# Two encoder layers in one kernel: two more of eleven swiglu blocks by seven products, the other blocks divided into steps

## The chip, the cores and the metric

The kernel runs on one core of a Trainium2 chip. The metric is the device time of one execution in microseconds. Before the change the median of three runs was 2283.49 us (2281.22 to 2284.84).

## The reference

Two layers on 256 tokens of width 2048, all in float32. Layer 0 mixes tokens with chunked gated linear attention (GLA), layer 1 with an indexer and top-k attention (DSA); each mixer is followed by a swiglu whose inner width is 5632, and a last RMSNorm ends it.

```python
def swiglu(h, w1, w3, w2):
    return (jax.nn.silu(h @ w1) * (h @ w3)) @ w2

for i in range(DEPTH):
    x = x + mixer(rmsnorm(x, norm_mix[i]))
    x = x + swiglu(rmsnorm(x, norm_ffn[i]), ffn_w1[i], ffn_w3[i], ffn_w2[i])
return rmsnorm(x, norm_final)
```

## The kernel before, in words

**One product.** A float32 product is made of three passes in the type float32r: each operand is split into a high part and a rest, and high x high, high x rest and rest x high are added up in a PSUM bank. A weight tile of 512 rows by 512 columns (1 MB) is split by `split_w` (L132): ScalarE (ACT) casts it into `wh` (L136), VectorE (DVE) subtracts that from it into `wl` (L137). Both have three buffers. Raw weights come by SyncE's queue (SP) into `raw`, which has four. A chunk is what one such tile feeds.

**A swiglu block.** The inner width is cut into eleven blocks of 512 columns. The 256 tokens are two tiles of 128; the contraction over 2048 is cut into two halves. `plain` (L450) computes a block of w1 and then of w3 in eight chunks, 24 matmuls of 128x512 each, 192 in all (L464), into three PSUM banks of the pool `acc`. `pair` (L369) takes the same block of w1 and w3 as the two column halves of one matrix product and the token tiles and contraction halves as the others, so that the scheme of Strassen and Winograd gives it in seven products of 24 matmuls (L394), 168 in all. The products are named after the form of the activations that is stationary: A11, F5, F3, F6, F7, A12, N22. The weights change between products: `va` holds w1's first half, `vb` w3's. After A11 has split `va`, VectorE adds `vb` to it (`plus`, L406); after F5 has split that, a DMA adds w3's second half to it in place (`plus_dma`, L409, issued by POOL); F3 splits `vc`, w3's second half from `raw`, and adds it to `vb` (L406); F6 splits `va` and a second accumulating DMA adds w1's second half; F7 splits `vb`, A12 splits `vd`, w1's second half from `raw`, and N22 splits `va`. Every product goes by two chunks. `va` and `vb` live in two places that change roles from pair to pair (`homes`, `turn`, L413): the next pair's `va` is loaded where this pair's `vb` was, its `vb` where this pair's `va` was.

**Down projection.** `pieces` (L477) multiplies two finished blocks by w2, in eight steps of one chunk and 24 matmuls (L490 to L492), into two banks of the pool `ms`; after every second step VectorE adds both banks to x (L497).

**Order.** `ffn` (L500) runs b = 0 to 10. Blocks 2, 4, 6, 8 and 10 are pairs, the other six plain. `pair` yields after each product and once more at its end, and at each yield one step of the down projection of the two blocks before it runs; beside plain blocks none is left to run. A finished block is transposed by `split_t` (L209), which goes on the deque `side` and is taken up by `tick` between matmuls. What is left over, block 10, goes to `residual` (L348) after the swiglu, which multiplies it by w2 and, in layer 0, prepares the next layer; in layer 1 the last quarter of it is `gemm_tail` (L140), one token tile after the other, and the final norm follows.

A planner puts the instructions of each engine into one queue ahead of the run, in the program's order as far as its own costs say that operands and buffers are ready, and fills in the semaphores. So an instruction can stand before one that precedes it in the program.

Of the kernel before, what the change touches and what calls it, by code (L numbers as in the profile page):

```python
# [12 lines left out]
F32 = mybir.dt.float32  # L13
# [6 lines left out]
P = 128  # L20
SEQ = 256
# [34 lines left out]
def trunk(  # L56
# [38 lines left out]
    cols = cst.tile([P, 72], F32, name="cols")  # L95


    sm.tile([P, 24], F32, tag="pad", bufs=1, name="pad")

    def gains(c0, srcs):  # L100

# [262 lines left out]
    def flush():  # L364
        while side:
            tick()


    def pair(nrm, wa, wb, c0, turn, done):  # L369

        def src(w, j, c):
            r = j * 1024 + c * 512
            return w[r:r + 512, c0:c0 + NB].rearrange("(k p) n -> p k n", p=P)

        def load(w, j, homes):
            o = []
            for c, (pool, tag, bufs) in enumerate(homes):
                raw = pool.tile([P, 4, NB], F32, tag=tag, bufs=bufs, name=tag)  # L380
                nc.sync.dma_start(raw, src(w, j, c))
                o.append(raw)
            return o

        def product(acc, raws, form, start, stop, then=None):
            for c in range(2):
                wh, wl = split_w(raws[c])
                if then is not None:
                    then(c)
                hi, lo = nrm.forms[form]  # L390
                for j in range(4):
                    k = 4 * c + j
                    for i, (l_, r_) in enumerate(((hi, wh), (hi, wl), (lo, wh))):
                        nc.tensor.matmul(acc, l_[:, k, :], r_[:, j, :], start=start and k == i == 0,  # L394
                                         stop=stop and k == 7 and i == 2, skip_group_check=not start)
                    if j % 2:
                        tick()

        def bank():
            return acc_p.tile([P, NB], F32, tag="acc", name="acc")  # L400

        def sums(tag):
            return nrm.pool.tile([P, NB], F32, tag=tag, bufs=1, name=tag)

        def plus(dst, other):
            return lambda c: nc.vector.tensor_add(dst[c], dst[c], other[c])  # L406

        def plus_dma(dst, w, j):
            return lambda c: nc.gpsimd.dma_start(dst[c], src(w, j, c), accum_op=ALU.add)  # L409

        fz = nrm.pool
        stream = [(wp, "raw", RAW)] * 2
        homes = [((fz, "v0", 1), (fz, "v1", 1)), ((fz, "v2", 1), (res, "g3", 1))]  # L413
        va = load(wa, 0, homes[turn])
        vb = load(wb, 0, homes[1 - turn])
        b1 = bank()
        product(b1, va, "A11", True, True, plus(va, vb))
        s1 = sums("s1")
        nc.scalar.copy(s1, b1)
        yield  # L420
        b2 = bank()
        product(b2, va, "F5", True, True, plus_dma(va, wb, 1))
        y = sums("y")
        nc.vector.tensor_sub(y, b2, s1)
        yield
        vc = load(wb, 1, stream)
        product(b2, vc, "F3", False, True, plus(vb, vc))
        yield
        b3 = bank()
        product(b3, va, "F6", True, True, plus_dma(va, wa, 1))  # L430
        w = sums("w")
        nc.vector.tensor_sub(w, b3, s1)
        yield
        product(b3, vb, "F7", False, True)
        nc.vector.tensor_add(w, w, b2)
        nc.vector.tensor_add(y, y, b3)
        yield
        vd = load(wa, 1, stream)
        product(b1, vd, "A12", False, True)
        done("11", b1)  # L440
        done("12", w)
        yield
        product(b3, va, "N22", False, True)
        nc.vector.tensor_sub(s1, s1, b3)
        done("21", s1)
        done("22", y)
        yield
        yield

    def plain(nrm, ws, c0, done):  # L450

        for q, w in zip("12", ws):
            acc = [acc_p.tile([P, NB], F32, tag="acc", name="acc") for _ in range(3)]
            for g in range(4):
                raw = wp.tile([P, 4, NB], F32, tag="raw", bufs=RAW, name="raw")
                nc.sync.dma_start(raw, w[g * NB:(g + 1) * NB, c0:c0 + NB].rearrange("(k p) n -> p k n", p=P))
                wh, wl = split_w(raw)
                for bank, form, start, stop in ((0, "A11", True, True), (1, "F7", True, True)) if g < 2 else \
                        ((0, "A12", False, True), (2, "N22", True, True)):
                    hi, lo = nrm.forms[form]  # L460
                    for j in range(4):
                        k = 4 * (g % 2) + j
                        for i, (l_, r_) in enumerate(((hi, wh), (hi, wl), (lo, wh))):
                            nc.tensor.matmul(acc[bank], l_[:, k, :], r_[:, j, :], start=start and k == i == 0,  # L464
                                             stop=stop and k == 7 and i == 2, skip_group_check=not start)
                        if j % 2:
                            tick()
                if g == 1:
                    s1 = nrm.pool.tile([P, NB], F32, tag="s1", bufs=1, name="s1")
                    nc.scalar.copy(s1, acc[0])  # L470
                    nc.vector.tensor_add(s1, s1, acc[1])
                    yield
            nc.vector.tensor_sub(s1, s1, acc[2])
            done("1" + q, acc[0])
            done("2" + q, s1)

    def pieces(w, parts):  # L477

        for n in range(NG):
            acc = [ms_p.tile([P, NB], F32, tag="ms", name=f"down{t}") for t in range(NT)]  # L480
            for gi, (hi, lo, r0) in enumerate(parts):
                raw = wp.tile([P, 4, NB], F32, tag="raw", bufs=RAW, name="raw")
                nc.sync.dma_start(raw, w[r0:r0 + 512, n * NB:(n + 1) * NB].rearrange("(k p) n -> p k n", p=P))
                wh, wl = split_w(raw)
                for k in range(4):
                    start = gi == 0 and k == 0
                    last = gi == len(parts) - 1 and k == 3
                    for t in range(NT):
                        ts_ = slice(t * P, (t + 1) * P)
                        nc.tensor.matmul(acc[t], hi[:, k, ts_], wh[:, k, :], start=start, stop=False)  # L490
                        nc.tensor.matmul(acc[t], hi[:, k, ts_], wl[:, k, :], start=False, stop=False)  # L491
                        nc.tensor.matmul(acc[t], lo[:, k, ts_], wh[:, k, :], start=False, stop=last)  # L492
                    if k % 2:
                        tick()
                if gi == len(parts) - 1:
                    for t in range(NT):
                        nc.vector.tensor_add(x[t][n], x[t][n], acc[t])  # L497
                yield

    def ffn(layer, nrm):  # L500

        w1, w3, w2 = ffn_w1[layer], ffn_w3[layer], ffn_w2[layer]
        sc = {}
        parts = []
        down = deque()
        for b in range(DFF // NB):
            us = [None] * NT

            def done(q, v):
                t = int(q[0]) - 1  # L510
                if q[1] == "1":
                    us[t] = cm.tile([P, NB], F32, tag="u", name="u")
                    nc.scalar.activation(us[t], v, AF.Silu, scale=sc["r"][:, t:t + 1])
                else:
                    nc.vector.scalar_tensor_tensor(us[t], us[t], sc["r"][:, t:t + 1], v, op0=ALU.mult, op1=ALU.mult)

            for slot, _ in enumerate(pair(nrm, w1, w3, b * NB, b // 2 % 2, done) if b in range(2, 11, 2) else plain(nrm, (w1, w3), b * NB, done)):
                if b == 0 and slot == 0:
                    flush()
                    r = nrm.rstd()  # L520
                    sc["r"] = r
                while down:
                    try:
                        next(down[0])
                        break
                    except StopIteration:
                        down.popleft()
            hi, lo = hi_lo(b % 3)
            side.append(split_t(us, hi, lo))
            parts.append((hi, lo, b * NB))  # L530
            if b % 2:
                down.append(pieces(w2, parts))
                parts = []
        while down:
            for _ in down.popleft():
                pass
        return w2, parts


# [554 lines left out]
```

## Time and profile before

| | |
|---|---|
| median of three runs | 2283.49 us |
| the profiled execution | 2283.89 us |
| its span, first to last instruction | 2282.1 us |
| PE, DVE, ACT, POOL busy | 2254.4, 1499.3, 1127.5, 79.3 us |
| mean granted TensorE clock | 0.998 of full speed |
| moved by DMA | 468.18 MB, mean 205 GB/s |

PE is TensorE's matmuls, PEld its weight loads, SP SyncE's queue. A matmul's recorded duration is longer than the distance to the next start, since matmuls overlap; lengths of stretches are more reliable than sums of durations. A "releaser" is what ended a wait, told from semaphores.

### The profile page before, as it was taken

What the parts mean: (1) busy time and instruction counts of PE and PEld (TensorE: products, weight loads), DVE (VectorE), ACT (ScalarE), POOL (GpSimd) and SP (SyncE); (2) the same over time, 40 slices, a digit from 0 to 9 for tenths busy, and PEclk for the clock granted to TensorE, in tenths of its full rate; (3) what the DMA queues carried; (4) which work ended last, traced back from release to release, by engine and by line L of the source; (5) the groups of instructions that cost most, each with busy time, mean ns of one, the idle gap of its engine ahead of it and who ended that gap; (6) DMA issues with size and microseconds to landing.
All of it is one profiled execution on the core that took longest, in us unless ns stands there. A gap on an engine that the chain in (4) does not pass through costs nothing.

```text
span 2282.1 us, 25208 instructions
## 1 busy us (share of the span) xinstructions
PE 2254.4 (99%) x10343; PEld 1856.3 (81%) x10343; DVE 1499.3 (66%) x1254; ACT 1127.5 (49%) x1026; POOL 79.3 (3%) x131
## 2 busy tenths in 40 slices
PE   9999999999999999999999999999999999999998
PEld 7888888887888888887888888888888788888886
DVE  6546456577676867776655755556675867777676
ACT  5545355444454545545544544455454454545454
POOL 0000000000000000000100000000000000000000
PEclk9999999999999999999999999999999999999999
DMA  8555465759495876857554555457496786949593
GB/s 286 168 171 188 127 233 187 237 160 302 147 299 199 216 263 184 289 159 218 173 182 148 184 166 166 165 186 240 147 277 234 193 273 174 296 146 305 166 239 111
DMA packets 242098, 468.18 MB, mean 205 GB/s; under 512 B 7816, under 2 KB 20448, under 8 KB 241856
## 3 DMA queue, kind: packets, MB, share of 16 engines
q1 hardware_dynamic: 219856, 423.33, 54.4%
q0 software_dynamic: 21120, 41.95, 10.7%
q8 instruction: 81, 1.33, 0.2%
q10 hardware_dynamic: 1008, 1.31, 0.2%
q14 instruction: 33, 0.27, 0.0%
HBM read 464.43 MB, written 2.12 MB: 204 GB/s over the span
## 4 chain that ended last, share of the span: by engine, by line
PE 68%; issue 20%; DMA 5%; DVE 4%; ACT 2%; POOL 0%; POOLq 0%; ACTq 0%; SPq 0%
PE acc L464 14%; PE acc L204 11%; PE acc L202 11%; PE acc L203 11%; PE acc L394 8%; PE down L490 3%; PE down L491 3%; DMA g<-in_ffn_w 3%; PE down L492 3%; DVE wl L137 2%; DMA v<-in_ffn_w 2%; ACT wh L136 1%; DVE v L406 1%; PE tr L216 1%; PE trq L825 0%
## 5 line engine op out<-in xcount | busy, mean ns | idle before, releaser
L137 DVE TENSOR_TENSOR wl<-raw,wh 128x2048 fp32r<-128x2048 f32 x217 | 496.8, 2290 | 261.3 <-ACT wh L136 261.3
L136 ACT CAST wh<-raw 128x2048 fp32r<-128x2048 f32 x217 | 415.7, 1915 | 474.1 <-PE down L492 176.6
L193 DVE TENSOR_TENSOR wl<-raw,wh 128x2048 fp32r<-128x2048 f32 (+3 forms) x147 | 317.8, 2164 | 276.4 <-ACT wh L192 276.3
L192 ACT CAST wh<-raw 128x2048 fp32r<-128x2048 f32 (+3 forms) x147 | 265.5, 1809 | 230.8 <-PE acc L204 194.6
L202 PE MATMUL acc<-wh,hh 128*128 128x512 f32 (+3 forms) x832 | 326.8, 393 | 0.0
L204 PE MATMUL acc<-wh,hl 128*128 128x512 f32 (+3 forms) x832 | 318.4, 383 | 0.0
L203 PE MATMUL acc<-wl,hh 128*128 128x512 f32 (+3 forms) x832 | 317.0, 381 | 0.5 <-DVE wl L193 0.5
L491 PE MATMUL down<-wl,g 128*128 128x512 f32 x640 | 249.2, 389 | 0.0
L492 PE MATMUL down<-wh,g 128*128 128x512 f32 x640 | 249.0, 389 | 0.0
L490 PE MATMUL down<-wh,g 128*128 128x512 f32 x640 | 247.5, 389 | 0.0
L137 DVE TENSOR_TENSOR wl<-v,wh 128x2048 fp32r<-128x2048 f32 x72 | 164.3, 2287 | 44.6 <-ACT wh L136 44.6
L136 ACT CAST wh<-v 128x2048 fp32r<-128x2048 f32 x72 | 137.4, 1908 | 97.0 <-PE acc L394 39.2
L203 PEld LDWEIGHTS acc<-wl,hh 128*128 128x128 f32 x832 | 156.6, 188 | 30.3 <-issue 1.7
L204 PEld LDWEIGHTS acc<-wh,hl 128*128 128x128 f32 x832 | 156.2, 188 | 30.6
L202 PEld LDWEIGHTS acc<-wh,hh 128*128 128x128 f32 x832 | 156.4, 188 | 29.0 <-issue 1.9
L464 PE MATMUL acc<-wh,fhA 128*128 128x512 f32 x384 | 152.2, 396 | 0.1
L464 PE MATMUL acc<-wh,flA 128*128 128x512 f32 x384 | 150.4, 392 | 0.0
L464 PE MATMUL acc<-wl,fhA 128*128 128x512 f32 x384 | 149.8, 390 | 0.0
L490 PEld LDWEIGHTS down<-wh,g 128*128 128x128 f32 x640 | 120.1, 188 | 25.5
L491 PEld LDWEIGHTS down<-wl,g 128*128 128x128 f32 x640 | 120.1, 188 | 25.3
L492 PEld LDWEIGHTS down<-wh,g 128*128 128x128 f32 x640 | 120.1, 188 | 25.0
L394 PE MATMUL acc<-wl,fhF 128*128 128x512 f32 x320 | 127.8, 399 | 8.4 <-DVE wl L137 8.4
(281 smaller groups left out, 3617.0 us busy)
## 6 DMA issues: line engine op xcount, KB each, us to landing
raw<-in_ffn_w SPq DMA_DIRECT2D x224, 1024.0 KB, 5.2
raw<-in_dsa_w_in SPq DMA_DIRECT2D x48, 1024.0 KB, 5.0
raw<-in_gla_w_in SPq DMA_DIRECT2D x40, 1024.0 KB, 5.1
v<-in_ffn_w SPq DMA_DIRECT2D x30, 1024.0 KB, 6.9
v<-in_ffn_w POOLq DMA_DIRECT2D x28, 1024.0 KB, 8.9
raw<-in_gla_w_out SPq DMA_DIRECT2D x16, 1024.0 KB, 5.0
raw<-in_dsa_w_out SPq DMA_DIRECT2D x16, 1024.0 KB, 4.9
g<-in_ffn_w POOLq DMA_DIRECT2D x12, 1024.0 KB, 13.7
```

What stands on the lines that cost most here:

```text
L136: nc.scalar.copy(wh, raw)
L137: nc.vector.tensor_sub(wl, raw, wh.bitcast(F32))
L192: a = nc.scalar.copy(wh[:, sl, :n], raw[:, sl, :n])
L193: v = nc.vector.tensor_sub(wl[:, sl, :n], raw[:, sl, :n], wh[:, sl, :n].bitcast(F32))
L202: nc.tensor.matmul(acc[t][:, :n], hi[:, k, ts_], wh[:, k, :n], start=start, stop=False)
L203: nc.tensor.matmul(acc[t][:, :n], hi[:, k, ts_], wl[:, k, :n], start=False, stop=False)
L204: nc.tensor.matmul(acc[t][:, :n], lo[:, k, ts_], wh[:, k, :n], start=False, stop=last)
L394: nc.tensor.matmul(acc, l_[:, k, :], r_[:, j, :], start=start and k == i == 0, stop=stop and k == 7 and i == 2, skip_group_check=not start)
L464: nc.tensor.matmul(acc[bank], l_[:, k, :], r_[:, j, :], start=start and k == i == 0, stop=stop and k == 7 and i == 2, skip_group_check=not ...
L490: nc.tensor.matmul(acc[t], hi[:, k, ts_], wh[:, k, :], start=start, stop=False)
L491: nc.tensor.matmul(acc[t], hi[:, k, ts_], wl[:, k, :], start=False, stop=False)
L492: nc.tensor.matmul(acc[t], lo[:, k, ts_], wh[:, k, :], start=False, stop=last)
```

## The change

In `ffn`, block 0 stays plain. Then seven turns follow, each a pair with eight steps in its yields: pairs 2, 3, 4, 6, 7, 8 and 10. In the turns of pairs 2, 6 and 10 the steps are a whole plain block (1, 5, 9), divided by the new `plain_steps`; in the turns of 3, 4, 7 and 8 they are `pieces` of the two oldest finished blocks. Three blocks (8, 9, 10) are left for `residual`. `plain_steps` does 24 matmuls a step, as `plain` does, uses the two `ms` banks and keeps its sums in the place (`g0` to `g2`) that later takes its transposed block; its part `turned`, left out below, makes the eight transposes in two ticks and then ACT's and VectorE's split of both halves.

In `pair`, the product A12 moves from sixth place to fourth, with its load of `vd`; two yields without a product in between now stand between F7 and N22, one after N22 (before: none, and two). The sum `w` is finished right after F6.

The tile `pad` grows by 16 floats, so that everything allocated behind it (the zone that holds `va`, `vb` and the forms) moves by 64 bytes.

```diff
-    sm.tile([P, 24], F32, tag="pad", bufs=1, name="pad")
+    sm.tile([P, 40], F32, tag="pad", bufs=1, name="pad")
@@ pair
         product(b2, vc, "F3", False, True, plus(vb, vc))
         yield
+        vd = load(wa, 1, stream)
+        product(b1, vd, "A12", False, True)
+        done("11", b1)
+        yield
         b3 = bank()
         product(b3, va, "F6", True, True, plus_dma(va, wa, 1))
         w = sums("w")
         nc.vector.tensor_sub(w, b3, s1)
+        nc.vector.tensor_add(w, w, b2)
+        done("12", w)
         yield
         product(b3, vb, "F7", False, True)
-        nc.vector.tensor_add(w, w, b2)
         nc.vector.tensor_add(y, y, b3)
         yield
-        vd = load(wa, 1, stream)
-        product(b1, vd, "A12", False, True)
-        done("11", b1)
-        done("12", w)
         yield
         product(b3, va, "N22", False, True)
...
         done("22", y)
         yield
-        yield
@@ new
+    def plain_steps(ws, b, forms, sc, ready):
+        flat = res.tile([P, 4 * NB], F32, tag=f"g{b % 3}", name="early")
+        us = [flat[:, t * NB:(t + 1) * NB] for t in range(NT)]
+        s1 = flat[:, NT * NB:(NT + 1) * NB]
+        for q, w in enumerate(ws):
+            acc = [ms_p.tile([P, NB], F32, tag="ms", name="half") for _ in range(2)]
+            for gi in range(4):
+                raw = wp.tile([P, 4, NB], F32, tag="raw", bufs=RAW, name="raw")
+                nc.sync.dma_start(raw, w[gi * NB:(gi + 1) * NB, b * NB:(b + 1) * NB].rearrange("(k p) n -> p k n", p=P))
+                wh, wl = split_w(raw)
...
+                if gi == 1:
+                    nc.scalar.copy(s1, acc[0])
+                    nc.vector.tensor_add(s1, s1, acc[1])
+                    acc[1] = ms_p.tile([P, NB], F32, tag="ms", name="half")
+                if gi < 3:
+                    yield
+            r = sc["r"]
+            if q == 0:
+                nc.scalar.activation(us[0], acc[0], AF.Silu, scale=r[:, 0:1])
+                nc.vector.tensor_sub(s1, s1, acc[1])
+                nc.scalar.activation(us[1], s1, AF.Silu, scale=r[:, 1:2])
+                yield
+            else:
+                nc.vector.scalar_tensor_tensor(us[0], us[0], r[:, 0:1], acc[0], op0=ALU.mult, op1=ALU.mult)
+                nc.vector.tensor_sub(s1, s1, acc[1])
+                nc.vector.scalar_tensor_tensor(us[1], us[1], r[:, 1:2], s1, op0=ALU.mult, op1=ALU.mult)
...
@@ ffn
+        for turn, (b, inner) in enumerate(((2, 1), (3, None), (4, None), (6, 5), (7, None), (8, None), (10, 9))):
+            if inner is None:
+                two, parts[:2] = parts[:2], []
+                work = pieces(w2, two)
+            else:
+                work = plain_steps((w1, w3), inner, nrm.forms, sc, ready)
+            us = [None] * NT
+            made = None
+            for slot, _ in enumerate(pair(nrm, w1, w3, b * NB, 1 - turn % 2, gate(us))):
+                if inner is None and slot == 0:
+                    assert all(r0 in ready for _, _, r0 in two)
+                made = next(work)
+            if inner is not None:
+                parts.append(made)
+            block(b, us)
```

## Rows read from the trace of the kernel before

**Rows 1.** Page, part 1: busy time, share, instructions of each engine
```profile
PE 2254.4 (99%) x10343; PEld 1856.3 (81%) x10343; DVE 1499.3 (66%) x1254; ACT 1127.5 (49%) x1026; POOL 79.3 (3%) x131
```

**Rows 2.** Windows: start:end, length, engines' busy time, PEclk, DMA share, GB/s
```profile
485.49:570.11 84.62, 83.23 (x369) 68.22 (x368) 66.05 (x43) 44.69 (x27) 5.42 (x4) 1.00 0.88 261
570.11:614.99 44.88, 44.88 (x201) 36.85 (x200) 26.68 (x18) 18.86 (x14) 0.00 (x0) 1.00 0.51 164
...
491.91:502.86 10.95, 10.95 (x49) 9.01 (x48) 10.76 (x8) 6.25 (x4) 1.52 (x1) 1.00 0.72 165
...
476.64:502.08 25.44, 25.44 (x117) 20.86 (x116) 25.37 (x15) 12.78 (x9) 1.52 (x1) 1.00 0.33 86
```

**Rows 3.** Windows of L394 alone: one F5; F6 of the ten pairs
```profile
497.37:502.86 5.49, 5.49 (x24) 4.32 (x23) 1.00 0.88 138
...
1034.06:1043.62 9.56, 7.62 (x24) 5.38 (x23) 0.82 0.91 201
...
sum 68.16, PE 59.58 PEld 43.54; mean PE 5.96 PEld 4.35
```

**Rows 4.** Waits of TensorE's weight loads: us in total, times, longest
```profile
PEld acc L394 <- DVE wl L137: 12.5, 10, 2.1
...
PEld acc L202 <- ACT g L218: 3.7, 2, 1.8
...
PEld acc L204 <- DVE g L219: 1.7, 2, 1.0
```

**Rows 5.** Timeline of POOL in the first pair: start, us, instruction, idle before
```profile
496.14 1.52 POOL L409 DMA_DIRECT2D v<-in_ffn_w  x1 [95.16 <-DVE wl L137]
505.38 1.31 POOL L409 DMA_DIRECT2D g<-in_ffn_w  x1 [7.72 <-DVE y L424]
```

**Rows 6.** Chain of waits in order of time, first pair: start, us, what
```profile
505.38 13.99 DMA g<-in_ffn_w
```

**Rows 7.** DMA packets between 496 and 523 us
```profile
DMA packets 3349, 6.65 MB, mean 246 GB/s; under 512 B 112, under 2 KB 112, under 8 KB 3347
```

**Rows 8.** The accumulating DMAs of L409, all forty
```profile
DMA to landing us min/median/max: 8.3/9.1/15.1
```

**Rows 9.** Timeline of SyncE's queue, around the first pair's N22
```profile
550.01 0.37 SPq L381 DMA_DIRECT2D v<-in_ffn_w  x1
553.35 0.37 SPq L381 DMA_DIRECT2D g<-in_ffn_w  x1
```

**Rows 10.** Page, part 6: loads of va and vb, KB each, us to landing
```profile
v<-in_ffn_w SPq DMA_DIRECT2D x30, 1024.0 KB, 6.9
```

**Rows 11.** Timeline of ACT, around the first pair's N22
```profile
556.69 1.92 ACT L136 CAST wh<-raw 128x2048 fp32r<-128x2048 f32 x1 [0.83 <-PE acc L394]
```

**Rows 12.** Timeline of DVE: first pair's begin, its N22, the kernel's end
```profile
478.97 2.29 DVE L406 TENSOR_TENSOR v<-v,v 128x2048 f32<-128x2048 f32 x1
481.30 2.29 DVE L406 TENSOR_TENSOR v<-v,raw 128x2048 f32<-128x2048 f32 x1
...
486.37 0.68 DVE L473 TENSOR_TENSOR s<-s,acc 128x512 f32<-128x512 f32 x1
486.97 2.29 DVE L406 TENSOR_TENSOR g<-g,v 128x2048 f32<-128x2048 f32 x1
489.17 0.74 DVE L515 SCALAR_TENSOR_TENSOR u<-u,rstd,s 128x512 f32<-128x512 f32 x1
489.83 2.28 DVE L137 TENSOR_TENSOR wl<-raw,wh 128x2048 fp32r<-128x2048 f32 x1
...
553.26 1.37 DVE L497 TENSOR_TENSOR x<-x,down 128x512 f32<-128x512 f32 x2
...
558.64 2.29 DVE L137 TENSOR_TENSOR wl<-raw,wh 128x2048 fp32r<-128x2048 f32 x1 [0.46 <-ACT wh L136]
...
2273.91 0.68 DVE L1055 TENSOR_TENSOR x<-x,acc 128x512 f32<-128x512 f32 x1
```

**Rows 13.** Timeline of PE at the kernel's end
```profile
2272.66 0.40 PE L155 MATMUL acc<-wh,g 128*128 128x512 f32 x1
```

More of the change, by code (lines that the diff above doesn't have):

```diff
@@ L475, in plain, with turned @@
             done("2" + q, s1)
+    def plain_steps(ws, b, forms, sc, ready):
[8 more added lines that the diff above has]
+                wh, wl = split_w(raw)
+                for bank, form, start, stop in ((0, "A11", True, True), (1, "F7", True, True)) if gi < 2 else \
+                        ((0, "A12", False, True), (1, "N22", True, True)):
+                    hi, lo = forms[form]
+                    for j in range(4):
+                        k = 4 * (gi % 2) + j
+                        for i, (l_, r_) in enumerate(((hi, wh), (hi, wl), (lo, wh))):
+                            nc.tensor.matmul(acc[bank], l_[:, k, :], r_[:, j, :], start=start and k == i == 0,
+                                             stop=stop and k == 7 and i == 2, skip_group_check=not start)
+                        if j % 2:
+                            tick()
+                if gi == 1:
[14 more added lines that the diff above has]
+                nc.vector.scalar_tensor_tensor(us[1], us[1], r[:, 1:2], s1, op0=ALU.mult, op1=ALU.mult)
+        def turned():
+            tr = []
+            for kk in range(2):
+                tr.append(tr_p.tile([P, 2, SEQ], F32, tag="tr", name="tr"))
+                for t in range(NT):
+                    for k in range(2):
+                        c = (2 * kk + k) * P
+                        nc.tensor.transpose(tr[kk][:, k, t * P:(t + 1) * P], us[t][:, c:c + P], ident)
+                if kk == 0:
+                    yield
+            hi, lo = hi_lo(b % 3)
+            for kk in range(2):
+                sl = slice(2 * kk, 2 * kk + 2)
+                nc.scalar.copy(hi[:, sl, :], tr[kk])
+                nc.vector.tensor_sub(lo[:, sl, :], tr[kk], hi[:, sl, :].bitcast(F32))
+            part[:2] = hi, lo
+            ready.add(b * NB)
+            yield
+        part = [None, None, b * NB]
+        side.append(turned())
+        yield part
@@ L504, in ffn, with block, turned, gate @@
         parts = []
-        down = deque()
-        for b in range(DFF // NB):
-            us = [None] * NT
+        ready = set()
+        def block(b, us):
+            def turned():
+                yield from split_t(us, hi, lo)
+                ready.add(b * NB)
+            hi, lo = hi_lo(b % 3)
+            side.append(turned())
+            parts.append((hi, lo, b * NB))
+        def gate(us):
             def done(q, v):
@@ L515, in done @@
                     nc.vector.scalar_tensor_tensor(us[t], us[t], sc["r"][:, t:t + 1], v, op0=ALU.mult, op1=ALU.mult)
[L517 to L536, printed above, removed]
+            return done
+        us = [None] * NT
+        for slot, _ in enumerate(plain(nrm, (w1, w3), 0, gate(us))):
+            if slot == 0:
+                flush()
+                sc["r"] = nrm.rstd()
+        block(0, us)
+        for turn, (b, inner) in enumerate(((2, 1), (3, None), (4, None), (6, 5), (7, None), (8, None), (10, 9))):
[4 more added lines that the diff above has]
+                work = plain_steps((w1, w3), inner, nrm.forms, sc, ready)
+            us = [None] * NT
+            made = None
[6 more added lines that the diff above has]
+            block(b, us)
         return w2, parts
```

## The prediction

> **What bounds the kernel now.** I read the page's busy shares first, then windows over one pair block and the plain block behind it, then PE's waits, and last the queues of VectorE, POOL and SyncE around one pair. PE is busy for 2254.4 of 2282.1 us, VectorE for two thirds of it [rows 1]: the end is the number of matmuls times their pitch, plus what PE loses to late operands. One product (24 matmuls) takes 5.49 us, one product and one step between products together 10.95, so a step 5.46 [rows 2, 3]. A pair with its eight steps takes 84.62 us, of which VectorE works 66.05; the plain block behind it takes 44.88, of which VectorE works 26.68 [rows 2]. So now every pair is followed by a stretch in which VectorE has 40% to spare, and the next pair begins with splits and additions done ahead.
>
> The only wait of PE that repeats in the swiglu is in each pair's fourth product, F6: ten stretches of 24 matmuls take 68.16 us where 10 x 5.49 = 54.9 is due, so 13.3 us are lost; in the worst the granted clock fell to 0.82 of full speed (half speed, 1.2 GHz, in part of it) after PE had waited 2.1 us [rows 3, 4]. Its cause stands in the POOL queue: the accumulating transfer of the second half is issued at 505.38, when the one of the first half has landed, and lands 13.99 us later, at 519.37; only then come ACT's cast and VectorE's subtraction for F6's second half, while PE stands [rows 5, 6].
>
> **The change part by part.** *Matmuls.* A plain block is eight products' worth (192 matmuls), a pair seven (168). Each layer turns two plain blocks into pairs, two layers: 4 x 5.49 = 22.0 us less. The four steps per layer that a down projection leaves go to the residual behind it (three parts instead of one, 288 matmuls for 96; the pairs lose 192), and the divided plain blocks keep their 192: nought.
>
> *A12 fourth.* F5, which frees the sum for the first accumulation, and F6, which needs it, had one product and two steps between them, 16.4 us; now two and three, 27.4. The transfers need the same 23 us behind F5's first split (496.14 to 519.37 [rows 5, 6]), so they land 9 us before F6's second cast is due. A12 brings its own two loads into that time, and three MB more are due before F6; the row of that stretch moves 6.65 MB in 27 us at 246 GB/s [rows 7], so 3 MB are 13 us at worst: with a fair share between the queues the wait is gone, with none it stays. I take it as gone: -13.3 (ends 0 and -13.3).
> The second accumulation now has F6, F7 and three steps before N22 (27.3 us from F6's start; before 32.8 from F6's start plus its stall). From F6's start, its first half is issued at -3.7 (as now, a split runs that far ahead), lands at +5, its second lands at +19 to +20 (landing at most 15.1 [rows 8]); N22's second cast must start by +26. Hidden, with 6 us to spare; if the cover went, the price would be that of F6 now.
>
> *Next pair's loads.* The second operand of the next pair goes where this pair's N22 reads, so SyncE waits for N22's second split: 553.35 in a pair whose N22 begins at 553.74 [rows 9]. Such loads land after 6.9 us in the median [rows 10], so at 6.5; A11 begins 10.9 us after N22, and VectorE comes to that addition at about 14 (below). Nought, even if contention doubles the landing; SyncE's raw loads, queued behind it, are up to four ahead of their use, and wait no longer than this one does.
>
> *VectorE where pair follows pair.* This is what the change adds. There are 12 such borders (six a layer), none before. Count from N22's start = 0; s7 the step behind it, A11 at 10.93, next step s0 at 16.42, F5 at 21.9. Three buffers hold split weights, so a split starts when the third chunk before it has been used; ACT's cast starts 0.2 us later and VectorE 2.14 after the release, as when N22's first half, done at 556.48, is followed by 556.69 and 558.64 [rows 11, 12]. A11's first half is released at 2.74, so VectorE takes it at 4.88. From there the queue holds, at the pitches of rows 12: split 2.2, s1's subtraction 0.6, first addition of the pair 2.2, the gate's last product 0.66, split of A11's second half 2.2, the two sums of s7 into x 1.36, second addition 2.2, split for s0 2.29: 13.7, ended at 18.6. PE wants it at 16.65: 1.9 us late. Where the steps were a plain block (four borders), the sums into x give way to product, subtraction, product, 1.92: 2.5 us late. Before, the same s0 split ended at 492.11 with PE wanting it at 492.14, one pitch behind s0's start at 491.91 [rows 2, 12]: there was no room, though A11's first addition and one of F3's had run from 6.5 us ahead of A11, the latter out of the program's order. Which order the planner picks decides: with s0's split ahead of the second addition it ends at 16.4 and costs nothing; with F3's two additions in front too (4.4 us), 6 us. Ends 0 and 6.3 a border; I take the program's order, as the rows before show for these four instructions: 8 x 1.9 + 4 x 2.5 = +25.2.
> Over a whole pair VectorE has room: 22 splits and 4 additions at 2.2, some 20 small ones, 71 of 82 us, so what is late at a border is made good by A12.
>
> The Trainium skill (Perfetto Trace Analysis, Optimization Strategy) says that a kernel whose most contended engine changes over time may gain by interleaving its regimes, and its section on the most contended engine goes by occupancy. By that rule 71 of 82 us would leave VectorE no limit and the borders would cost nought, 2244.6 in all; the window over a pair's begin, where VectorE is busy 25.37 of 25.44 us [rows 2], speaks for the local view.
>
> *Residual behind the swiglu.* PE waits there for the last block's transposed halves, 3.7 + 1.7 us in two residuals [rows 4]. Now the first part is an older block, which covers the copies; but the divided block's last chain (product, subtraction, product) stands between the last step and its transposes, 0 to 2.2 us each, by whether PE goes on with ready matmuls. I take half: -5.4 + 2.2 = -3.2 (ends -5.4 and 0).
>
> *End.* The last token tile's addition starts at 2273.91, after the first tile's scaling, though its last matmul began at 2272.66 and lasted 0.40 [rows 12, 13]. With 36 matmuls (8.2 us) instead of 12 in the second half, the first tile's work is over: -0.8.
>
> *64 bytes.* Products (stationary from the moved zone) run at 228.8 ns a matmul, steps (from an unmoved one) at 227.5 [rows 2, 3]. Nothing shows that place matters; bound by that difference over 3888 matmuls, 5 us either way, taken as 0.
>
> *Sum.* -22.0 - 13.3 - 3.2 - 0.8 + 25.2 = -14.1. The profiled execution took 2283.89 (span 2282.1 and 1.8 around it), 0.4 over the median 2283.49: 2283.9 - 14.1 = 2269.8, on the median's footing 2269.
>
> **Rivals.**
> *VectorE is in time at the borders.* For: the planner already moves additions out of order [rows 12], and one swap of order suffices. Against: it moved them early into idle time, which a border lacks. Without the 25.2: 2244.6, 2245.
> *F6 goes on waiting.* For: the 16 DMA engines are the limit in that stretch; both halves are serial in the POOL queue, and the second takes 14 us against 9 for the first, with two raw loads in flight [rows 6, 7]. Against: 11 us more. Price 13.3: 2283. The Trainium skill (DMA: Bandwidth & Descriptors, Issuing engines are not separate DMA queues) says that transfers of all issuers run on the same 16 engines and interleave. The trace agrees (9 against 14 us); by that rule alone A12's loads take their share of the 11 us gained, and this rival is the result.
> *VectorE later still, slower than before.* Place: the same 12 borders, with both additions of F3 in front of a split that PE waits for, 4.4 us each: 12 x 4.4 = 52.8 against gains of 39.3, 2297. It decides from 3.3 us a border on, sooner if such waits pull the clock down: the one of 2.1 us cost 9.56 - 5.49 = 4.1 in all [rows 3]. For: 25 us of VectorE without a gap already. Against: F3's additions are needed only by F7, and a late PE gives VectorE time.
>
> **How the numbers follow.** Forecast 0.46, in time at the borders 0.26, slower 0.14, F6 waits on 0.08, else 0.06. The forecast's own range is 1 to 3 us a border, 2256 to 2282. The range reaches to the second case and most of the way to the slower one: 2244 to 2291. A measurement of this kernel can tell 0.2%, 4.6 us: faster is below 2279. Most of the forecast (0.40), all of the second case and 0.05 of the others: 0.71. Within 0.2%: 0.04 of the forecast, most of the case with F6's wait: 0.10. Slower 0.19.
>
> **What would show it.** Fourteen pairs of 168 matmuls and 96 fewer in all. No wait before F6; POOL's second transfer landed some 9 us before its cast. At each border one wait of PE for VectorE's split, at the first step behind A11, of about 2 us, longer behind the divided blocks. VectorE's busy time up by 24 splits and 16 additions, 92 us, less what the plain blocks' gates save. If PE's waits at the borders sum to under 8 us, the queue count was wrong; over 40 us, so was the order. A fall of the granted clock in the swiglu stretches would be a cost that I left out.

## The result, and the profile after

The changed kernel takes 2261.23 us in the median of four runs (2259.76 to 2262.72), the kernel before, beside it on the same chip, 2282.65 (2281.22 to 2284.84): a ratio of 0.9903, 95% interval 0.9891 to 0.9914. It is faster by 21 us; the forecast was 2269, inside a range from 2244 to 2291. The profiled execution took 2262.72 us with a span of 2260.9, 21.2 less than before, and the accounts below are made on spans. In one of the experiments (the zone 320 bytes on) one of four executions took 3189.4 us at a mean granted clock of 0.654, and its median is that of the other three.

Page, part 1, of the kernel after: busy us, share of the span and instructions of each engine.

```profile
PE 2226.0 (98%) x10247; PEld 1834.7 (81%) x10247; DVE 1576.4 (70%) x1282; ACT 1169.4 (52%) x1046; POOL 100.1 (4%) x147
```

Against [rows 1] these are the 96 matmuls fewer that were forecast, and 77 us more of VectorE. TensorE's busy time fell by 28.4 us; 96 matmuls at 227 ns are 21.8 of it, and 4.7 are F6's, which was busy for 59.58 us where 54.9 was due [rows 3]. What the others do can't be read from the busy time of matmuls that overlap; the distances of their starts, below, show it.

What TensorE's weight loads waited for, kernel after: engine, tile, line, releaser: us in total, times, longest.

```profile
PEld down L552 <- DVE wl L137: 20.2, 17, 2.0
PEld half L494 <- DVE wl L137: 11.6, 10, 2.0
...
PEld down L551 <- DVE x L558: 3.3, 14, 0.3
...
PEld acc L394 <- DVE wl L137: 0.4, 1, 0.4
```

All three waits of [rows 4] have gone: F6 (12.5 us in ten) has none (the one of 0.4 us left at L394 is in an A12), and the two at the residual's start (3.7 and 1.7) are in no row. In their place stand 27 waits in the steps between products, a down projection's (L552) or a divided block's (L494): one of 1.6 to 2.0 us at each of the twelve borders, eight of 0.4 to 0.5 behind F5, seven of 0.5 to 1.1 behind A12. The releaser is the same as before, VectorE's split `wl`; the place has changed.

### The profile page after: what moved, and what is told of

The parts are those of the page before. It is cut to its first block, busy times and chain, and to the rows that moved or that the text cites. A ratio compares the mean times of both kernels' runs of the same rounds, so it can differ in the third digit from the quotient of the medians.

```text
span 2260.9 us, 25126 instructions
## 1 busy us (share of the span) xinstructions
PE 2226.0 (98%) x10247; PEld 1834.7 (81%) x10247; DVE 1576.4 (70%) x1282; ACT 1169.4 (52%) x1046; POOL 100.1 (4%) x147
## 4 chain that ended last, share of the span: by engine, by line
PE 81%; DVE 11%; DMA 3%; ACT 2%; issue 2%; SPq 0%; POOL 0%; POOLq 0%; ACTq 0%
PE acc L394 15%; PE acc L202 12%; PE acc L204 12%; PE acc L203 12%; PE half L494 9%; DVE wl L137 4%; PE down L552 4%; PE down L553 4%; PE down L551 4%; DMA raw<-in_ffn_w 3%; PE acc L464 3%; DVE v L406 2%; ACT wh L136 2%; DVE g L406 1%; DVE x L558 1%
## 5 line engine op out<-in xcount | busy, mean ns | idle before, releaser
L136 ACT CAST wh<-raw 128x2048 fp32r<-128x2048 f32 x187 | 358.0, 1915 | 439.4 <-PE down L553 164.3
L137 DVE TENSOR_TENSOR wl<-raw,wh 128x2048 fp32r<-128x2048 f32 x187 | 426.8, 2289 | 204.1 <-ACT wh L136 203.9
L202 PE MATMUL acc<-wh,hh 128*128 128x512 f32 (+3 forms) x832 | 325.5, 391 | 0.0
L204 PE MATMUL acc<-wh,hl 128*128 128x512 f32 (+3 forms) x832 | 317.3, 381 | 0.0
L137 DVE TENSOR_TENSOR wl<-v,wh 128x2048 fp32r<-128x2048 f32 x102 | 232.8, 2287 | 24.5 <-ACT wh L136 24.4
L136 ACT CAST wh<-v 128x2048 fp32r<-128x2048 f32 x102 | 195.2, 1913 | 76.6 <-PE acc L394 43.4
L552 PE MATMUL down<-wl,g 128*128 128x512 f32 x512 | 201.3, 393 | 13.7 <-DVE wl L137 13.5
L553 PE MATMUL down<-wh,g 128*128 128x512 f32 x512 | 199.6, 390 | 0.0
L551 PE MATMUL down<-wh,g 128*128 128x512 f32 x512 | 198.3, 391 | 0.0
L204 PEld LDWEIGHTS acc<-wh,hl 128*128 128x128 f32 x832 | 156.3, 188 | 29.5
L202 PEld LDWEIGHTS acc<-wh,hh 128*128 128x128 f32 x832 | 156.5, 188 | 28.6 <-issue 1.9
L394 PE MATMUL acc<-wh,fhF 128*128 128x512 f32 x448 | 174.6, 390 | 0.0
L394 PE MATMUL acc<-wl,fhF 128*128 128x512 f32 x448 | 174.3, 389 | 0.0
L394 PE MATMUL acc<-wh,flF 128*128 128x512 f32 x448 | 174.3, 389 | 0.0
L202 PE MATMUL acc<-wh,g 128*128 128x512 f32 x424 | 167.0, 394 | 0.0
L203 PE MATMUL acc<-wl,g 128*128 128x512 f32 x424 | 165.8, 391 | 0.0
L204 PE MATMUL acc<-wh,g 128*128 128x512 f32 x424 | 165.6, 391 | 0.0
L552 PEld LDWEIGHTS down<-wl,g 128*128 128x128 f32 x512 | 96.1, 188 | 39.2 <-DVE wl L137 20.2
```

What stands on the lines that cost most here:

```text
L136: nc.scalar.copy(wh, raw)
L137: nc.vector.tensor_sub(wl, raw, wh.bitcast(F32))
L202: nc.tensor.matmul(acc[t][:, :n], hi[:, k, ts_], wh[:, k, :n], start=start, stop=False)
L203: nc.tensor.matmul(acc[t][:, :n], hi[:, k, ts_], wl[:, k, :n], start=False, stop=False)
L204: nc.tensor.matmul(acc[t][:, :n], lo[:, k, ts_], wh[:, k, :n], start=False, stop=last)
```

## The experiments

All times are medians; a ratio stands to the kernel before, run beside it. That kernel took 2282.65 to 2284.40 us beside the different ones, so a difference between two that were not run side by side is good to some 2 us.

### A12 fourth, and nothing else

The kernel before with only this part of the change: A12 between F3 and F6, the second sum finished behind F6, its yields as in the change.

```diff
         product(b2, vc, "F3", False, True, plus(vb, vc))
         yield
+        vd = load(wa, 1, stream)
+        product(b1, vd, "A12", False, True)
+        done("11", b1)
+        yield
         b3 = bank()
...
-        vd = load(wa, 1, stream)
-        product(b1, vd, "A12", False, True)
...
-        yield
         yield
```

> The kernel before with A12 as fourth product and nothing else (blocks and zone as before). Theory (the accumulating transfer lands in time once A12 and a step stand before F6): F6's ten stretches take 55 us in place of 68, 13 us less, some 2269 us; the second transfer lands over 5 us before F6's second cast. Rival (A12's loads take from the transfer what the two stretches give): F6 still waits 0.5 us or more a pair, 2277 us or more.

Measured: 2272.93 us (2272.16 to 2274.3), ratio 0.9947 (0.9933 to 0.9961), against 2284.40 beside it: -11.5. F6 of the ten pairs, windows of L394 alone as in [rows 3], the last two pairs and the sum:

```profile
2070.49:2075.98 5.49, 5.49 (x24) 4.32 (x23) 1.00 0.91 165
2198.49:2203.98 5.49, 5.49 (x24) 4.32 (x23) 1.00 1.00 179
sum 54.91, PE 54.89 PEld 43.19; mean PE 5.49 PEld 4.32
```

The sum is 54.91, ten times 5.49, where it was 68.16: the wait has gone whole, and with it the fall of the clock. The span lost only 10.9 us, for a new small wait came with the new order. Two steps now stand together between F7 and N22, and in the second of them TensorE's weight loads wait for VectorE's sums into x:

```profile
PEld down L490 <- DVE x L497: 3.6, 14, 0.3
```

By the distances of its starts TensorE loses 2.1 us there.

### 64 bytes alone, on the kernel before

```diff
-    sm.tile([P, 24], F32, tag="pad", bufs=1, name="pad")
+    sm.tile([P, 40], F32, tag="pad", bufs=1, name="pad")
```

> The kernel before with the zone moved by 64 bytes and nothing else. Theory (place): pitch of the products and of the plain blocks falls from 229.1 to 227.2 ns, 3984 x 1.9 ns = 7.6 us less, some 2275 us; F6's waits stay. Rival (place plays no part): 2282.6 us, no change.

Measured: 2288.94 us (2284.70 to 2292.65), ratio 1.0019 (1.0009 to 1.0030). Both theories missed: it is slower. The matmuls did become faster, as the theory wanted; F6's wait took more than that back. Waits of TensorE's weight loads, then windows of L394 alone over three F6 (start:end, length, PE and PEld busy, PEclk, DMA share, GB/s) with the sum over ten, and the two waits in the first of them, all in this kernel:

```profile
PEld acc L394 <- DVE wl L137: 20.8, 10, 2.1
...
PEld acc L394 <- ACT wh L136: 3.4, 6, 0.9
```

```profile
775.88:786.45 10.57, 8.24 (x24) 5.72 (x23) 0.74 0.95 223
908.77:915.74 6.97, 5.74 (x24) 4.24 (x23) 1.00 1.00 236
...
1942.56:1952.12 9.56, 7.59 (x24) 5.38 (x23) 0.82 0.91 201
...
sum 83.25, PE 64.86 PEld 46.24; mean PE 6.49 PEld 4.62
```

```profile
779.26 0.19 PEld L394 LDWEIGHTS acc<-wh,fhF 128*128 128x128 f32 x1 [0.92 <-ACT wh L136]
781.59 0.28 PEld L394 LDWEIGHTS acc<-wl,fhF 128*128 128x128 f32 x1 [2.14 <-DVE wl L137]
```

Ten F6 take 83.25 where 10 x 5.44 = 54.4 is due: 28.9 us lost, 13.3 before. Two things make up the 15.6 us more. In four of the ten the granted clock fell to half behind the waits; by the clock's records TensorE ran at half speed for 17.1 us in all (3.4 before), half of which is lost. And the waits are longer, counted on the weight loads 24.2 us (20.8 + 3.4) for 13.0, 1.1 us more a pair. Of that 1.1 TensorE's own gain is the small part: between F5 and F6 it saves 48 matmuls x 1.9 ns = 0.1 us. The transfers came later: the second one before F6 lands after 14.3 us in the mean of ten (13.6 in the kernel before), and is issued 9.3 us behind the first (9.1). In its time 2.2 of SyncE's loads are in flight in the mean, 2.0 before; whether that slows it, or the moved place to which it writes, no run separates. Against 15.6 us more at F6 stand 7.6 saved, and the profiled span is 7.5 longer, the median 4.5. A cost or gain "of 64 bytes" was no constant: it depends on what TensorE runs into.

### Both together on the kernel before

A12 fourth and 64 bytes, without the added pairs and divided blocks.

```diff
-    sm.tile([P, 24], F32, tag="pad", bufs=1, name="pad")
+    sm.tile([P, 40], F32, tag="pad", bufs=1, name="pad")
@@ pair
         product(b2, vc, "F3", False, True, plus(vb, vc))
         yield
+        vd = load(wa, 1, stream)
+        product(b1, vd, "A12", False, True)
...
```

> The kernel before with A12 as fourth product and the zone moved by 64 bytes; blocks as before (five pairs a layer). Theory (the zone alone gave nothing because F6 waited for a transfer that doesn't get faster; with that wait gone the shorter pitch counts in full): 2272.9 - 7.6 = 2265 us, no wait before F6. Rival (the zone's move makes the transfers slower, and so costs wherever they are near the limit): F6 waits again, 2270 us or more. Against the changed kernel's 2261 this run also tells what the four added pairs and the divided blocks are worth by themselves: 4 us by the theory, not the 22 us of their matmuls.

Measured: 2266.45 us (2265.01 to 2267.75), ratio 0.9922 (0.9908 to 0.9936), as the theory had it. With F6's wait gone (no wait at L394 is left), the same 64 bytes give 6.5 us (2272.93 to 2266.45; the kernels before, beside them, differ by 0.7). The rival's premise holds in part: the second transfer before F6 lands after 14.4 us in the mean of ten, 13.5 without the 64 bytes. It is early all the same. From here to the full change is only 5.2 us, though it has four pairs more, 22 us of matmuls: the rest of these 22, and what the residual and the end gain, is what the borders cost.

### The place given back, and other places

The changed kernel with the zone back in its old place, then at 32, 128 and 320 bytes behind it.

```diff
-    sm.tile([P, 40], F32, tag="pad", bufs=1, name="pad")
+    sm.tile([P, 24], F32, tag="pad", bufs=1, name="pad")     # old place
+    sm.tile([P, 32], F32, tag="pad", bufs=1, name="pad")     # 32 bytes behind it
+    sm.tile([P, 56], F32, tag="pad", bufs=1, name="pad")     # 128
+    sm.tile([P, 104], F32, tag="pad", bufs=1, name="pad")    # 320
```

The old place:

> The changed kernel with the zone back where it was (pad of 24 floats). In the changed kernel the matmuls of the swiglu whose stationary operand lies in the zone follow each other every 227.2 ns, before every 229.1. Theory (the place of the zone sets that): products back to 5.49 us, 3888 matmuls x 1.9 ns = 7.5 us more than the changed kernel, some 2269 us. Rival (something else in the change, as the order of the products or the missing plain stretches, made the pitch shorter): pitch stays 227.2, time stays at 2261 us.

Measured: 2269.18 us (2267.59 to 2269.66), ratio 0.9929 (0.9915 to 0.9943): 8.0 us more than the changed kernel (5.9 by the two ratios).

32 and 128 bytes, one run each:

> The changed kernel with the zone 32 bytes behind its old place (pad of 32 floats) in place of 64. Theory (the pitch goes with the place in steps of 64 bytes or more): pitch of the products 229.1 or 227.2 ns like one of the two. Rival (it goes gradually with the place): a pitch in between or above. Time 2261 to 2269 us.

> The changed kernel with the zone 128 bytes behind its old place (pad of 56 floats) in place of 64. Theory (what counts is the place within 128 bytes): pitch back at 229.1 ns, 2269 us. Rival (the old place alone was bad): 227.2 ns, 2261 us.

Measured: 8905.44 us at 32 bytes, with matmuls of some 840 ns pitch from the first instruction on, those included whose operands don't lie in the zone; 2291.16 us at 128 bytes. So both were run again, with a fourth place:

> The changed kernel with the zone 32 bytes behind the old place instead of 64, as in the single run before, repeated. That run took 8905 us with a matmul every 840 ns from its first instruction on, also where neither operand lies in the zone. If the place is the cause, this one takes about 8900 again. The rival, a disturbance of that one run: about 2261 to 2275 us, with a pitch between 227 and 233 ns at the products.

> The changed kernel with the zone 128 bytes behind the old place, repeated with timing. If the pitch of 233.4 ns of the single run is the place's doing: 233.4 again at products and plain steps, 4.9 us a thousand matmuls more than at 64 bytes, some 2288 to 2293 us, slower than the kernel before. The rival, that it was that run: 227 to 229 ns and 2261 to 2270 us.

> The changed kernel with the zone 320 bytes behind the old place, 256 behind the new one. If the pitch goes by the place within 256 bytes, it is that of the 64-byte place: 227.2 ns at the products, 2261 us. The rival, that it goes by something else of the place: another pitch, at 229.1 (the old place) 2269 us, at 233.4 about 2290.

Measured: at 32 bytes 2289.20 us (2288.74 to 2289.79), ratio 1.0024 (1.0014 to 1.0035); at 128 bytes 2290.08 (2289.86 to 2290.76), ratio 1.0028 (1.0018 to 1.0039); at 320 bytes 2262.12, ratio 0.9902 (0.9886 to 0.9919). Eight executions at 32 bytes now agree, so the 8905 us were that one execution, not the place; what slowed it is not known, and nothing rests on it. The rest is the place. One product of a pair without a wait, window of L394 alone, at 0, 128 and 320 bytes:

```profile
634.70:640.20 5.50, 5.50 (x24) 4.32 (x23) 1.00 1.10 248
```

```profile
641.50:647.10 5.60, 5.60 (x24) 4.32 (x23) 1.00 1.09 253
```

```profile
634.92:640.36 5.44, 5.44 (x24) 4.32 (x23) 1.00 1.10 247
```

The mean distance between starts at L394 (gaps of over 300 ns left out) is 229.2 ns at 0, 233.2 at 32, 227.2 at 64, 233.5 at 128 and 227.2 at 320 bytes. Of the two operands of these matmuls only the stationary one, a form, lies in the zone; the weights `wh` and `wl` are in `wp`, allocated ahead of `pad`. The mixers' projections at L202 to L204, whose stationary `hh` and `hl` are allocated behind `pad` too, go the same way: 229.4 ns at 0, 227.9 at 64, 233.3 at 128 bytes. Nothing else differs between these kernels, and at 32 and 128 bytes the whole gain of the change is gone: they are 0.2 to 0.3% slower than the kernel before. 64 and 320 bytes, 256 apart, agree; that the place counts within 256 bytes fits, and one pair of places doesn't prove it. What in the memory makes the difference was not found.

### The second addition behind the step's split

To test the borders: in the changed kernel A11's second addition into `vb` is written behind the step that follows A11, so that VectorE takes that step's split first.

```diff
-        product(b1, va, "A11", True, True, plus(va, vb))
+        product(b1, va, "A11", True, True, lambda c: c or plus(va, vb)(0))
         s1 = sums("s1")
         nc.scalar.copy(s1, b1)
         yield
-        b2 = bank()
+        b2 = plus(va, vb)(1) and bank()
```

> The changed kernel, but each pair's second addition in A11 (second half of va plus vb) stands in the program behind the step that follows A11, so VectorE has that step's split in its queue ahead of it. Theory (at a border only the order in VectorE's queue makes the split late, by less than one addition): the waits of 1.7 us at the first step behind A11 go, 12 x 1.8 = 21 us less than the changed kernel, some 2240 us; waits behind F5 grow by less than 0.5 us each. Rival (VectorE has too much work there, whatever the order): the wait moves to F5's second half or to the step behind F5, 1 us or more each, and the time stays above 2252 us.

Measured: 2246.26 us (2244.71 to 2247.01), ratio 0.9829 (0.9814 to 0.9845): 15.0 us less than the changed kernel, by the order of two instructions of 2.3 us that are both still there. VectorE's timeline at the border (start, us, line, out<-in; a bracket would be idle time), first in the changed kernel, then in this one:

```profile
599.46 2.29 DVE L137 TENSOR_TENSOR wl<-raw,wh 128x2048 fp32r<-128x2048 f32 x1 [3.56 <-ACT wh L136]
601.95 2.29 DVE L137 TENSOR_TENSOR wl<-v,wh 128x2048 fp32r<-128x2048 f32 x1 [0.20 <-ACT wh L136]
604.16 0.68 DVE L445 TENSOR_TENSOR s<-s,acc 128x512 f32<-128x512 f32 x1
604.76 2.28 DVE L406 TENSOR_TENSOR v<-v,v 128x2048 f32<-128x2048 f32 x1
606.96 0.74 DVE L584 SCALAR_TENSOR_TENSOR u<-u,rstd,y 128x512 f32<-128x512 f32 x1
607.62 1.27 DVE L558 TENSOR_TENSOR x<-x,down 128x512 f32<-128x512 f32 x2
608.82 2.28 DVE L137 TENSOR_TENSOR wl<-g,wh 128x2048 fp32r<-128x2048 f32 x1
611.02 0.68 DVE L219 TENSOR_TENSOR g<-tr,g 128x512 fp32r<-128x512 f32 x1
611.62 2.28 DVE L406 TENSOR_TENSOR g<-g,v 128x2048 f32<-128x2048 f32 x1
613.83 0.69 DVE L219 TENSOR_TENSOR g<-tr,g 128x512 fp32r<-128x512 f32 x1
614.43 2.28 DVE L137 TENSOR_TENSOR wl<-raw,wh 128x2048 fp32r<-128x2048 f32 x1
```

```profile
607.59 2.29 DVE L137 TENSOR_TENSOR wl<-g,wh 128x2048 fp32r<-128x2048 f32 x1
609.79 0.69 DVE L219 TENSOR_TENSOR g<-tr,g 128x512 fp32r<-128x512 f32 x1
610.39 2.29 DVE L137 TENSOR_TENSOR wl<-raw,wh 128x2048 fp32r<-128x2048 f32 x1
612.61 0.69 DVE L219 TENSOR_TENSOR g<-tr,g 128x512 fp32r<-128x512 f32 x1
613.21 2.28 DVE L406 TENSOR_TENSOR g<-g,v 128x2048 f32<-128x2048 f32 x1
```

In the changed kernel the row at 611.62 is the addition that can wait (F5's second half needs it) and the one at 614.43 the split for which TensorE stands. Here the split starts at 610.39 and TensorE finds it done. Theory's 2240 was still missed by 6 us, for waits that remain (10.0 us in 16 and 6.4 in 9), now mostly at the step behind A12, three products later, where they grew from 5.6 us in seven to 12.7 in thirteen: in part the rival was right. Two rows of this kernel there, ACT's cast and TensorE's weight load:

```profile
642.58 1.91 ACT L136 CAST wh<-raw 128x2048 fp32r<-128x2048 f32 x1 [4.82 <-DMA raw<-in_ffn_w]
```

```profile
646.87 0.19 PEld L552 LDWEIGHTS down<-wl,g 128*128 128x128 f32 x1 [1.12 <-DVE wl L137]
```

The cast waits 4.8 us for a raw load, which could only be issued when F3's last addition had read its buffer (632.76) and landed 9.7 us later, beside the accumulating transfer and three more loads. By name the releaser is VectorE; behind it stands a DMA.

### The spare step ahead of A12

The last experiment's kernel with one of the two yields between F7 and N22 moved between F3 and A12, which gives that late load one step more.

```diff
         product(b2, vc, "F3", False, True, plus(vb, vc))
         yield
+        yield
         vd = load(wa, 1, stream)
...
         nc.vector.tensor_add(y, y, b3)
         yield
-        yield
         product(b3, va, "N22", False, True)
```

> The kernel of the addition behind the step, and the step without a product in between moved from between F7 and N22 to between F3 and A12. What is left there waits 0.5 to 2.1 us at the step behind A12, where a raw load that was issued late lands after 10 us, in the same stretch as an accumulating transfer and A12's own loads. Theory (the loads of F3, A12 and of three steps are too dense there; 5.4 us more between F3 and A12 relieve it): that wait falls under 0.3 us a pair, 8 to 12 us less, some 2236 us. Rival (N22 then waits for the second accumulation, which has 21.8 us in place of 27.3): a new wait of 0.5 us or more at N22, no gain, 2244 us or more.

Measured: 2235.26 us (2235.01 to 2235.57), ratio 0.9786 (0.9772 to 0.9799). Of the waits on VectorE's split in the down projection's steps this is left, with 0.7 us in four at L494. N22, where the rival wanted a new wait, has none:

```profile
PEld down L552 <- DVE wl L137: 3.8, 8, 0.8
```

This version beats both kernels: 26 us under the changed one, with the same instructions in another order.

## Why the prediction was right, and where it was off

The direction and the mechanism held. The place of the 64 bytes, put at nothing, was worth 9.8 us; the borders cost more than forecast, the residual less; and the forecast came out 8 us high.

**Matmuls.** Forecast -22.0; 96 fewer at 227 ns are -21.8.

**A12 fourth.** Forecast -13.3, F6's halves 9 us ahead of the second cast. Windows of L394 alone over F6 of the fourteen pairs after, the first, the third and the sum; then POOL's two transfers for the third and ACT's cast of the second half:

```profile
484.17:489.61 5.44, 5.44 (x24) 4.32 (x23) 1.00 1.04 188
...
654.66:660.10 5.44, 5.44 (x24) 4.32 (x23) 1.00 0.95 169
...
sum 76.16, PE 76.13 PEld 60.43; mean PE 5.44 PEld 4.32
```

```profile
619.56 1.29 POOL L409 DMA_DIRECT2D v<-in_ffn_w  x1 [42.08 <-issue]
629.57 1.30 POOL L409 DMA_DIRECT2D g<-in_ffn_w  x1 [8.71 <-DMA v<-in_ffn_w]
```

```profile
650.00 1.91 ACT L136 CAST wh<-g 128x2048 fp32r<-128x2048 f32 x1
```

The second transfer took 11.5 us here (13.99 in [rows 6]), landed at 641.1 and was 8.9 us early. The rival that F6 goes on waiting is out: A12's loads did share the 16 DMA engines, but at a time when 11 us more were to be had. The transfer before N22 (660.33, 11.3 us to landing) is hidden too, as forecast.

**Borders.** Forecast +25.2: 8 x 1.9 and 4 x 2.5, in the order of the program. TensorE's timeline at an ordinary border and at one behind a divided block:

```profile
614.34 0.61 PE L551 MATMUL down<-wh,g 128*128 128x512 f32 x2
614.80 0.39 PE L394 MATMUL acc<-wh,fhF 128*128 128x512 f32 x1
616.77 0.50 PE L552 MATMUL down<-wl,g 128*128 128x512 f32 x1 [1.58 <-DVE wl L137]
...
529.13 0.60 PE L216 MATMUL tr<-ident,u 128*128 128x128 f32 x4
529.49 0.48 PE L394 MATMUL acc<-wh,fhF 128*128 128x512 f32 x1
529.81 0.60 PE L216 MATMUL tr<-ident,u 128*128 128x128 f32 x4
531.76 0.50 PE L552 MATMUL down<-wl,g 128*128 128x512 f32 x1 [1.35 <-DVE wl L137]
```

From 614.80 to 616.77 are 1.97 us, 1.74 more than a matmul; behind divided blocks the last of the transposes starts 1.63 ahead, and transposes follow each other every 0.11, so 1.52 are lost. All twelve borders have such a gap: 8 x 1.75 + 4 x 1.52 = 20.1. The queue count had 13.7 us from the start of A11's first split to the end of the split that comes late; in VectorE's timeline of the changed kernel above it is 601.95 to 616.71, 14.8. What the count left out on VectorE (two rests of transposed halves, L219, 0.6 each) has its like on TensorE, where the transposes themselves stretch A11 from 5.5 to 6.4 us, so the difference came out right by luck, by two omissions. Behind a divided block VectorE is indeed later, by 0.7, but eight transposes fill part of the wait: the order of the two sizes was wrong. And "what is late at a border is made good by A12" was too kind: by the distances of TensorE's starts 9.1 us more than before go in small waits behind F5 and A12, and the experiment with the second addition shows that a raw load, held back by VectorE's late additions, is behind part of them. Another 1.6 go in the second of the two steps ahead of N22, where A12's move alone lost 2.1. Together 30.8 for 25.2. (The forecast's own range, 1 to 3 us a border, ends at 2280.6, where it has 2282.)

VectorE's share told nothing of this. The window over one whole pair, from A11 to A11:

```profile
608.00:693.00 85.00, 83.39 (x370) 68.09 (x369) 69.13 (x44) 44.86 (x27) 5.19 (x4) 1.00 0.84 247
```

(Start:end, length; PE, PEld, DVE, ACT and POOL busy; PEclk, DMA share, GB/s.) VectorE works 69 of 85 us and TensorE still stands at the border. By occupancy, the measure that the Trainium skill's page Perfetto Trace Analysis gives for it (Identifying the Most-Contended Engine) and the forecast weighed as a rival, VectorE has room to spare. The section Optimization Strategy of the same page of the Trainium skill goes on to the gaps of the engine that one optimizes for and to the instruction that ends them. The trace agrees with that: the 2.0 us of waiting at an ordinary border end with VectorE's split, and the experiment that reorders two of VectorE's instructions took 15.0 us off. The local row decides.

**Residual and end.** Forecast -3.2 and -0.8. The two waits of [rows 4] went whole, -5.4: the cover by an older block was enough, and the divided block's last chain cost 0.3 us a layer. At the end, VectorE's timeline and then TensorE's, kernel after:

```profile
2253.05 0.69 DVE L1127 TENSOR_TENSOR x<-x,acc 128x512 f32<-128x512 f32 x1 [4.45 <-PE acc L155]
```

```profile
2252.63 0.39 PE L155 MATMUL acc<-wh,g 128*128 128x512 f32 x1
```

The last addition follows its matmul (2252.63 + 0.39) at once, where it was 0.85 late [rows 12, 13]; from the last matmul's start to the span's end are 8.3 us, 9.4 before: -1.1.

**64 bytes: the step that failed.** "Nothing shows that place matters; bound by that difference over 3888 matmuls, 5 us either way, taken as 0." A product without a wait went from 5.49 to 5.44 us, the pitch from 229.1 to 227.2 ns: 3888 x 1.95 ns = -7.6 us, and the old place costs 8.0 when given back. The bound also left out the mixers' 2496 matmuls at L202 to L204 by `hh` and `hl`, which moved too: 559.0 us before, 556.8 after, 559.2 with the old place given back, so 2.2 us more. The difference from which the bound was made (1.3 ns between products and steps, [rows 2, 3]) was the effect itself, half hidden in rounding, and read as no evidence; and the bound was too narrow on the other side as well: 32 or 128 bytes cost 20 us against the old place (2289.20 and 2290.08 against 2269.18).

**The sum.** -21.8 (matmuls) -9.8 (pitch, 7.6 and 2.2) -13.3 (F6) +30.8 (borders, what is behind them, the steps ahead of N22) -5.4 (residual) -1.1 (end) = -20.6; the span lost 21.2. Of the 7.1 us by which the forecast of -14.1 fell short, the pitch is 9.8, residual and end are 2.5, and the borders took 5.6 back; 0.6 stays unexplained. That the total came within 8 us owes something to luck, since the two largest misses have opposite signs.

## What to carry to other kernels

In an engine's queue that is full for some 25 us, ask of every instruction in it who waits for it, and put the one that TensorE needs first: here one swap was worth 15 us, and one step moved another 11, where the matmuls saved gave 22. A faster stage ahead of a transfer that is late gains nothing until that transfer is early (here it even came later); so remove the wait before you count the speed. Where an edit moves buffers, read the matmul pitch before and after, in a product without waits, to a tenth of a nanosecond, and try some places: at two of the five tried here this change would have lost.

## What the runs showed of the hardware that was not expected

- The pitch of the same matmul (128x512, fp32r) depends on where its stationary operand lies in SBUF: 227.2, 229.2, 233.2 to 233.5 ns at five places of one zone, with TensorE at full granted clock in all. Products by untouched tiles (L551 to L553) stay at 227 to 228.
- Waits of 2.0 us at the borders left the granted clock at full speed in the changed kernel (1.00 in the window of a whole pair); in F6 of the kernel before with 64 bytes, two waits of 0.92 and 2.14 us in one product were followed by 0.74.
- An accumulating 1 MB transfer goes by its company rather than by its place in POOL's queue. In the two kernels the 52 that had less than one of SyncE's loads in flight beside them in the mean landed after 8.4 to 9.7 us, one of them after 10.3; the 44 that had 1.6 or more, all of them the second of two, after 11.3 to 15.6. The last pair's second one in each layer, with hardly a load beside it, is among the 52: 8.9 and 8.7 us before, 10.3 and 9.0 after. The order of products has to leave room for both transfers and the loads.
